# Where the steps of the mixers' generators are cut: behind each product's operands instead of behind its result

## The chip, the cores and the metric

The kernel runs on one core of a Trainium2 chip. The metric is the device time of one execution in microseconds; the median of three runs of the kernel before is 2840.65 us (2838.29 to 2842.82).

## What is computed

Two transformer-like blocks, one behind the other, on 1024 tokens of width 1024, in float32. The first block has three mixers beside each other, the second has two; each block ends with a feed-forward part. Cut to what matters here:

```python
def first_block(x, meta_tokens, w_in, ..., w_mlp_in, w_mlp_out, ln2_g, ln2_b):
    h = jnp.concatenate([meta, x], axis=1)                  # 16 + 1024 tokens
    proj = h @ w_in[l]
    q_a, f_a, i_a, g_a, z_b, xbc_b, dt_b, u_c = jnp.split(proj, split_idx, axis=-1)
    y_a = hgrn2_mixer(q_a, f_a, i_a, g_a, ...)              # 6 heads, a scan over chunks
    y_b = mamba2_mixer(z_b, xbc_b, dt_b, ...)               # 6 heads, a scan over chunks
    y_c = s5_mixer(u_c, ...)                                # complex diagonal scan, then a gate
    mixed = jnp.concatenate([y_a, y_b, y_c], axis=-1) @ w_out[l]
    h = layer_norm(ALPHA * h + mixed, ln1_g[l], ln1_b[l])
    ff = jnp.square(jax.nn.relu(h @ w_mlp_in[l])) @ w_mlp_out[l]
    h = layer_norm(ALPHA * h + ff, ln2_g[l], ln2_b[l])
    return h[:, N_META:]

def second_block(x, w_in, ...):
    qkv, z, beta_logit, a, sg_uv, gates = jnp.split(x @ w_in[l], pts, axis=-1)
    o_a = deltanet_branch(qkv, z, beta_logit, a, ...)       # gated delta rule, 4 heads
    o_b = spatial_gating_branch(sg_uv, ...)                 # 128-token blocks, 4 groups
    h = gate_a * (o_a @ w_branch_a[l]) + gate_b * (o_b @ w_branch_b[l])
    x = layer_norm_2(DEEPNORM_ALPHA * x + h @ w_out[l], ln1_g[l], ln1_b[l])
    up = causal_depthwise_conv_2(x @ w_up[l], conv_ffn[l])
    a_ff, b_ff = jnp.split(up, 2, axis=-1)
    return layer_norm_2(DEEPNORM_ALPHA * x + (jax.nn.silu(a_ff) * b_ff) @ w_down[l], ln2_g[l], ln2_b[l])
```

## The kernel before, in words

**Tiling.** Tokens are handled in two halves of 512 (the first with the 16 meta tokens in front). A dense product is made of 128 x 128 blocks of the stationary operand and 512 columns of the moving one, and each float32 product is three matmuls of high and low parts (`mm3`, line 233). A block of weights of 128 x 1024 comes in on SyncE's queue (`weights`, line 223): two buffers for the raw block, three each for the high part `wh` (made on ScalarE) and the low part `wl` (made on VectorE). The sums are in four PSUM banks called `ps`. The mixers have four PSUM banks of their own, `px` (`bank`, line 177), and 24 working tiles `f` (`t`, line 165).

**Generators.** Everything is written as Python generators: a dense part yields after each unit (24 matmuls of 512 columns where a tile is made, 12 where a down projection adds up), a mixer yields after each of its steps. `steps` (line 1553) runs a dense generator and puts steps of a mixer's generator among its own: after each dense step the pace `r` is added to a debt, and for each whole unit of debt one mixer step is issued. So with a pace below one some dense steps have no mixer step behind them, and with a pace above one several mixer steps come one right behind the other. `both` (line 1454) makes one step out of one step of each of several generators.

**The mixers' steps.** `hgrn` (line 354) goes over seven block sizes; for each one VectorE and ScalarE make an operand `M`, TensorE multiplies it, and the result is copied under a mask into the scores; then it yields. It yields nine times per pair of heads. `mamba` (line 564) yields after each of seven convolutions, twice for each chunk, and three times in its norm. `delta` (line 983) yields 18 times per head: among these, six times for the doubling of a triangular inverse (product, copy by ScalarE, product, masked copies by VectorE), twice for its refinement (product, VectorE, product, VectorE), and four times for the chain over the chunks (product, VectorE, product, ScalarE, product). `spatial` (line 1154) yields four times. Two heads of `delta` run in turns.

**Where they run.** HGRN2 and Mamba2 of the first half run beside S5 and beside the first projection `p1` (lines 1488 to 1490), and of the second half beside the first output projection and the first feed-forward part (lines 1497 and 1504). The delta rule and the spatial gate run beside the second block's projection `p2` and then beside a feed-forward part (lines 1517 and 1519 for the first half, 1534 and 1536 for the second).

**The order on an engine.** The calls give the program's order. When the tile context closes, a planner turns it into one list for each engine: it goes by program order but may take a later instruction first while an earlier one waits for its operands. [...]

The functions that the diff touches follow; `square` and `sums` (lines 537 and 546) make the two parts of a square and add them up over partitions by a product with ones.

Of the kernel before, what the change touches and what calls it, by code (L numbers as in the profile page):

```python
# [17 lines left out]
DRAM = bass.MemoryType.DRAM  # L18
# [11 lines left out]
# columns of the constant array  # L30
C_ID = 0
C_I10 = 128                   # 1024 times the identity
C_SGN = C_I10 + 128
C_TRI = C_SGN + 1
C_BLK = C_TRI + 128           # ones in the two diagonal 64-blocks
C_BAND = C_BLK + 128          # 64 zeros, 128 ones, 64 zeros
C_N = C_BAND + 256

# columns of the array of byte masks: the levels (only the columns in the second halves of their blocks),
# the same transposed (only the first halves), the diagonal, what is below it  # L40
# [6 lines left out]
# columns of the per-feature parameter array  # L47
P_HNW = 0
P_LB = 1
P_CW1 = P_LB + 3              # 7 x 4  # L50
# [4 lines left out]
P_CWQ = P_GB + 2              # 12 x 4  # L55
P_DNW = P_CWQ + 48
P_CWF = P_DNW + 1             # 44 x 3
# [4 lines left out]
# columns of the row array (the same on all partitions)  # L62
# [7 lines left out]
# order of the feature-major tiles of the first projection  # L70
U1 = dict(u=0, f=2, q=5, g=8, xbc=11, z=18)
NU1 = 21
# ... and of the second
# [4 lines left out]
class Op:  # L78
    """The hi and lo parts of an operand."""
# [8 lines left out]
class Kb:  # L88
# [54 lines left out]
    def mask(self, o, b=None):  # L143
        """A byte mask for four blocks of 128 columns, or for the halves of a level's blocks in them."""
        n = 128
        if b is not None:
            o += 64 * LEVELS.index(b)
            n = 64
        m = self.bm[:, o:o + n].rearrange("p (o t) -> p o t", o=1).to_broadcast([128, 4, n])
        return m if b is None else m.rearrange("p c (n b) -> p c n b", b=b)  # L150

    def halves(self, x, i, b):
        """The first or second halves of the blocks of 2 b columns."""
# [11 lines left out]
    def t(self, w, dt=F32):  # L165
        """A working tile of the mixers."""
        return self.mx.tile([128, 528], dt, tag="f", bufs=self.NF, name=self.nm("f"))[:, :w]

    def ta(self):
        """Two working tiles of 528 columns, out of the accumulators' tiles."""  # L170
# [16 lines left out]
    # ---------------------------------------------------------------- operands  # L187
# [18 lines left out]
    def xt(self, f=False):  # L206
        """A tile for the hi and lo parts of an operand; f: out of the mixers' tiles."""
# [8 lines left out]
    def split(self, src, w, f=False):  # L216
        """hi and lo parts of src [128, w]."""
# [5 lines left out]
    def weights(self, src, w):  # L223
        """hi and lo parts of a block of weights [128, w] in DRAM."""
# [8 lines left out]
    def mm3(self, out, a, b, start, stop):  # L233
        """out += a^T b with hi and lo parts."""
# [4 lines left out]
    def fm(self, out, w, xs, o, n, k0=0):  # L239
        """out [128 features, n tokens] from a unit of weights and the tiles xs."""  # L240
# [5 lines left out]
    # ---------------------------------------------------------------- first projection  # L246
# [91 lines left out]
    # ---------------------------------------------------------------- HGRN2  # L338
    def hgrn_pre(self):
        """ln(1 - lb) and lb, a column for each pair of heads."""  # L340
# [13 lines left out]
    def hgrn(self, p, h):  # L354
# [13 lines left out]
        # log f and k  # L368
# [19 lines left out]
        # scores  # L388
# [17 lines left out]
        # the queries of a level for both heads at once, each among zeros for the other's features  # L406
# [3 lines left out]
        for i, b in enumerate((16, 8, 4, 2, 1, 64, 32)):  # L410
# [11 lines left out]
            if b <= 16:  # L422
# [3 lines left out]
                for hd, o in ((0, 0), (1, 64)):  # L426
                    self.tt(y4[o:o + 64, :, hd, :].rearrange("p c (n b) -> p c n b", b=b), c5(M, o), c5(q, o), ALU.mult)
                ps = self.bank()
# [6 lines left out]
            else:  # L435
                self.tt(M4[:, :, 1, :], M4[:, :, 1, :], q4[:, :, 1, :], ALU.mult)

                def put(S, ps):
                    for j in range(0, 128, 2 * b):
                        self.act(S[j:j + b, :, j + b:j + 2 * b], ps[j:j + b, :, j + b:j + 2 * b])  # L440
                scores(M, M, b, put)
            yield
            if b == 1:
                di = self.mask(M_ID)
                scores(q, kr, 0, lambda S, ps: nc.vector.copy_predicated(out=S, mask=di, data=ps))
        yield
        # decays
# [12 lines left out]
        # kd with tokens on the partitions, and what each chunk adds to the state  # L460
# [5 lines left out]
        dS = self.bank().rearrange("p (c d) -> p c d", d=64)  # L466
        if h == 0:
# [3 lines left out]
            self.act(kTm[:16], b[:16, :128])  # L471
            for o in (0, 64):
# [4 lines left out]
        # the states before the chunks, both heads' on the diagonal  # L477
# [12 lines left out]
        self.hs[p] = last  # L490
        o_ = self.bank()
# [5 lines left out]
        yield  # L497
        # norm and gate
        g = self.t(512)
        nc.sync.dma_start(g, self.S1["g", p, h][:, 3 + R0:3 + NT])  # L500
        self.act(g, g, AF.Silu)
        ms = self.bank()
        self.sums(ms, [(self.blk, self.square(o_), slice(0, 128))])
# [7 lines left out]
    # ---------------------------------------------------------------- Mamba2  # L511
    def softplus(self, x, tag, w):
        """max(x, 0) + ln(1 + exp(-|x|)) in place; x is narrow."""
# [6 lines left out]
    def rows(self, x, n):  # L520
        """The sums over tokens up to each, a row in DRAM for each of the n columns of x."""
# [15 lines left out]
    def square(self, x):  # L537
        """The hi and lo parts of the square of x [128, 512]."""
# [7 lines left out]
    def sums(self, out, parts):  # L546
        """The sum of the products of ones (lhsT) and operands (p: their partitions)."""
# [4 lines left out]
    def conv4(self, src, NT, cw, cb, out):  # L552
        """Causal convolution of four taps, then silu."""
# [10 lines left out]
    def mamba(self, h):  # L564
# [8 lines left out]
        # dt and dA, with tokens on the partitions; the first six columns are the short chunk  # L573
        dt = self.s("m2dt", 30)
        d3 = dt.rearrange("p (c h) -> p c h", h=6)
        if h == 0:
# [9 lines left out]
                self.m2a.rearrange("p (o h) -> p o h", o=1).to_broadcast([128, 5 - c0, 6]), ALU.mult)  # L586
        b = self.bank()
# [5 lines left out]
        for c in range(c0, 5):  # L593
            L = 16 if c == 0 else 128
            t0 = 0 if c == 0 else R0 + 128 * (c - 1)
            # acum_t and exp(acum_t) on all partitions
# [24 lines left out]
            # x dt and B with tokens on the partitions  # L621
# [39 lines left out]
        # gate, norm  # L661
        sq = []
        for j in range(3):
# [4 lines left out]
            sq.append(self.square(Y[j]))  # L668
# [1045 lines left out]
```

## Time and profile before

| | us |
|---|---|
| median of three runs | 2840.65 |
| span of the profiled execution, first to last instruction | 2831.3 |
| TensorE matmul busy | 2768.6 (98%) |
| TensorE weight loads busy | 2262.4 (80%) |
| VectorE busy | 1793.7 (63%) |
| ScalarE busy | 1163.4 (41%) |
| GpSimd busy | 220.4 (8%) |

The profile gives no time for its own execution other than the span; the median of the runs is 9.4 us longer than this span. Names in its rows are the program's: `ps` and `px` are the two sets of PSUM banks, `f` a mixer's working tile, `xt` an activation in its two parts, `wh` and `wl` the parts of a block of weights, `ta` a tile of S5. Line 204 is the helper that issues every matmul, line 189 every activation, line 192 every two-operand VectorE instruction, so these are told apart by their tiles.

### The profile page before, as it was taken

To read this page: it belongs to the slowest core of one execution; us is meant where nothing else is said; L and a number is where in the kernel's file an instruction comes from. 1 tells how busy PE (TensorE), PEld (TensorE's weight loads), DVE (VectorE), ACT (ScalarE), POOL (GpSimd) and SP (SyncE) were. 2 spreads that over 40 slices of the span, in tenths; PEclk is the share of its full clock that TensorE was granted. 3 is DMA by queue.
4 is the path that set the end of the run, shared out by engine and by line. 5 is a ranking of instruction groups with operands and counts; after the bars stand their busy time and mean duration, and the time that the engine had idled before them with its cause. 6 is when DMAs were issued, how large, how long until landed. Compare 5 with 4: busy or idle time off the path is not lost.

```text
span 2831.3 us, 37337 instructions
## 1 busy us (share of the span) xinstructions
PE 2768.6 (98%) x14176; PEld 2262.4 (80%) x14176; DVE 1793.7 (63%) x3321; ACT 1163.4 (41%) x1810; POOL 220.4 (8%) x365
## 2 busy tenths in 40 slices
PE   8999999999999999999999999999999999999997
PEld 7788777777878878877788888888788888888886
DVE  7678768777756554386545675535867557675556
ACT  4334344444442353364323334435545334344432
POOL 3121000000001121010000001110100000000000
PEclk9999999999999999999999999999999999999999
DMA  7333462323344444333333455433244433342232
GB/s 220 122 94 93 139 202 81 113 89 113 106 147 149 157 144 133 123 101 123 105 104 119 142 184 166 126 126 130 79 136 140 149 104 101 107 139 92 97 96 75
DMA packets 138036, 351.55 MB, mean 124 GB/s; under 512 B 26779, under 2 KB 40641, under 8 KB 137857
## 3 DMA queue, kind: packets, MB, share of 16 engines
q1 hardware_dynamic: 113712, 295.34, 32.9%
q0 software_dynamic: 16672, 48.50, 5.0%
q10 hardware_dynamic: 7473, 5.34, 0.7%
q8 instruction: 111, 1.82, 0.3%
q14 instruction: 68, 0.56, 0.1%
HBM read 296.84 MB, written 51.69 MB: 123 GB/s over the span
## 4 chain that ended last, share of the span: by engine, by line
PE 81%; issue 7%; DVE 6%; DMA 2%; ACT 2%; POOL 1%; SPq 0%; DVEq 0%; POOLq 0%; ACTq 0%
PE ps L204 73%; PE px L204 7%; DVE f L192 2%; ACT f L189 1%; DVE wl L192 1%; PE px L1265 1%; DVE f L195 1%; DMA hx<-ev 1%; DMA wr<-in_w 0%; DVE acc L195 0%; DMA f<-rows 0%; DVE f L433 0%; ACT wh L189 0%; DVE ta L192 0%; ACT ev L189 0%
## 5 line engine op out<-in xcount | busy, mean ns | idle before, releaser
L204 PE MATMUL ps<-xt,wh 128*128 128x512 f32 (+1 forms) x3616 | 1117.0, 388 | 8.7 <-ACT wh L189 8.5
L192 DVE TENSOR_TENSOR wl<-wr,wh 128x1024 fp32r<-128x1024 f32 (+3 forms) x431 | 521.5, 1210 | 606.7 <-ACT wh L189 590.2
L189 ACT ACTIVATE wh<-wr 128x1024 fp32r<-128x1024 f32 (+3 forms) x431 | 452.3, 1050 | 898.4 <-PE ps L204 826.1
L204 PE MATMUL ps<-wh,xt 128*128 128x512 f32 (+3 forms) x2624 | 813.1, 384 | 4.7 <-ACT xt L189 4.4
L204 PEld LDWEIGHTS ps<-xt,wh 128*128 128x128 f32 x3616 | 665.9, 189 | 141.7 <-ACT wh L189 8.5
L204 PE MATMUL ps<-xt,wl 128*128 128x512 f32 (+1 forms) x1808 | 698.6, 387 | 3.9 <-DVE wl L192 3.9
L204 PEld LDWEIGHTS ps<-wh,xt 128*128 128x128 f32 (+1 forms) x2624 | 485.8, 188 | 99.9 <-ACT xt L189 6.9
L204 PE MATMUL ps<-wl,xt 128*128 128x512 f32 (+3 forms) x1312 | 502.2, 383 | 0.8 <-DVE wl L192 0.7
L204 PEld LDWEIGHTS ps<-xt,wl 128*128 128x128 f32 x1808 | 341.5, 189 | 72.8 <-DVE wl L192 5.5
L204 PE MATMUL ps<-f,wh 128*128 128x512 f32 x960 | 300.5, 394 | 0.0
L204 PEld LDWEIGHTS ps<-wl,xt 128*128 128x128 f32 (+1 forms) x1312 | 246.7, 188 | 46.5 <-DVE wl L192 2.0
L189 ACT ACTIVATE f<-f 128x512 f32<-128x512 f32 (+6 forms) x300 | 178.5, 613 | 200.6 <-DVE f L192 62.3
L204 PE MATMUL px<-f,f 128*128 128x128 f32 (+8 forms) x1832 | 201.4, 258 | 16.8 <-DVE f L192 10.2
L204 PEld LDWEIGHTS ps<-f,wh 128*128 128x128 f32 x960 | 180.3, 188 | 42.3
L189 ACT ACTIVATE ev<-ps 128x512 f32<-128x512 f32 (+4 forms) x303 | 169.6, 561 | 72.9 <-PE ps L204 67.1
L192 DVE TENSOR_TENSOR acc<-acc,ps 128x512 f32<-128x512 f32 x192 | 130.8, 683 | 95.8 <-PE ps L204 93.9
L204 PE MATMUL ps<-f,wl 128*128 128x512 f32 x480 | 189.4, 394 | 0.0
L204 PEld LDWEIGHTS px<-f,f 128*128 128x128 f32 (+2 forms) x1192 | 133.3, 180 | 52.9 <-issue 22.8
L192 DVE TENSOR_TENSOR f<-f,f 128x256 f32<-128x256 f32 (+5 forms) x244 | 128.6, 547 | 39.0 <-ACT f L189 37.0
L189 ACT ACTIVATE xt<-ev 128x512 fp32r<-128x512 f32 x131 | 82.3, 629 | 149.2 <-DVE ev L192 145.9
L195 DVE SCALAR_TENSOR_TENSOR ev<-ev,p,ev 128x512 f32<-128x512 f32 x176 | 132.2, 751 | 2.7 <-ACT ev L189 0.6
L192 DVE TENSOR_TENSOR xt<-ev,xt 128x512 fp32r<-128x512 f32 x124 | 85.9, 696 | 49.6 <-ACT xt L189 49.1
(223 smaller groups left out, 2046.9 us busy)
## 6 DMA issues: line engine op xcount, KB each, us to landing
wr<-in_w SPq DMA_DIRECT2D x93, 512.0 KB, 3.8
wr<-in_wup SPq DMA_DIRECT2D x88, 512.0 KB, 3.5
wr<-in_wmi SPq DMA_DIRECT2D x64, 512.0 KB, 3.6
wr<-in_wmo SPq DMA_DIRECT2D x64, 512.0 KB, 3.6
wr<-in_wdn SPq DMA_DIRECT2D x44, 512.0 KB, 3.5
wr<-in_wo SPq DMA_DIRECT2D x32, 512.0 KB, 3.7
Y<-f POOLq DMA_DIRECT2D x32, 256.0 KB, 2.6
ev<-Y SPq DMA_DIRECT2D x32, 256.0 KB, 3.6
```

The costliest lines, as they stand in the source:

```text
L189: self.nc.scalar.activation(out=out, in_=in_, func=func, **kw)
L192: self.nc.vector.tensor_tensor(out=out, in0=a, in1=b, op=op)
L195: self.nc.vector.scalar_tensor_tensor(out=out, in0=a, scalar=s, in1=b, op0=op0, op1=op1)
L204: self.nc.tensor.matmul(out, lhsT, rhs, start=start, stop=stop)
L1265: nc.tensor.transpose(b[:, 128 * t:128 * t + 128], acc[t][:, 128 * k:128 * k + 128], self.ident)
```

## The change

The yields are moved so that a mixer step begins with matmuls whose operands an earlier step made and ends with the VectorE and ScalarE work that makes the operands of the next one. Steps that held two or three dependent products are cut between them. The paces are raised in proportion to the new number of steps. No instruction is added or removed; some are issued earlier in program order (the squares of a norm, the row load and exponentials of `delta`, one product of the diagonal in `hgrn`). The diff also takes out comments and doc strings, which shifts line numbers and is left out here.

```diff
 def hgrn(self, p, h):
     for i, b in enumerate((16, 8, 4, 2, 1, 64, 32)):
         ...                                   # makes M (and y)
             if b <= 16:
+                yield
                 ps = self.bank()
                 ...                           # 4 products, masked copies
             else:
                 ...
+                yield
                 scores(M, M, b, put)
-            yield
-            if b == 1:
+            if i == 0:
                 di = self.mask(M_ID)
                 scores(q, kr, 0, ...)
-        yield
         ...                                   # decays, kd, qe
         self.tt(qe, q, eG[:, R0:NT], ALU.mult)
+        yield
         ...                                   # kd transposed into kT
-        dS = self.bank().rearrange("p (c d) -> p c d", d=64)
         if h == 0:
             ...
             self.act(kTm[:16], b[:16, :128])
+        yield
+        dS = self.bank().rearrange("p (c d) -> p c d", d=64)
+        if h == 0:
             for o in (0, 64):
                 self.mm(dS[o:o + 64, 0, :], kTm[:16, o:o + 64], vm[:16, o:o + 64])
         ...                                   # dS, the states S
         self.hs[p] = last
+        yield
         o_ = self.bank()
         ...                                   # products into o_
-        yield
         g = self.t(512)
         nc.sync.dma_start(g, ...)
         self.act(g, g, AF.Silu)
+        sq = self.square(o_)
+        yield
         ms = self.bank()
-        self.sums(ms, [(self.blk, self.square(o_), slice(0, 128))])
+        self.sums(ms, [(self.blk, sq, slice(0, 128))])
 def mamba(self, h):
     ...                                       # dt, dA
+        yield
         b = self.bank()
         self.mm(b[:, 0:30 - 6 * c0], self.tri, dA[:, wd])
     ...                                       # all chunks; gate and squares of the norm
+        yield
         for j in range(3):
             ...
 def glu(self, h):
     ...                                       # loads, gelu
+        yield
         for m in range(2):
 def delta(self, hd, h, cols):
     ...                                       # three convolutions
+        sq = [self.square(x) for x in (q, k)]
         yield
         ...                                   # norms of q and k, from sq
-        yield
         ...                                   # rows loaded, E, eR
         self.act(E, E, AF.Exp)
+        yield
         ...                                   # k and v transposed
-        yield
         ...                                   # k k^T, k q^T with decay
         yield
         ...
         for lb in (2, 4, 8, 16, 32, 64):
             ...
             self.act(self.halves(Z, 0, lb), nb(b))
+            yield
             ...                               # two products, masked copies
             yield
         for _ in range(2):
             ...
             self.stt(c3(R16), c3(b), 1024.0, k1024, mult, add)
+            yield
             ...
             yield
         for c in range(4):
             if S is not None:
                 self.mm(b[:, 0:128], k[:, s], S)
                 self.tt(R, vt[:, s], b[:, 0:128], sub)
+                yield
             b = self.bank()
             self.mm(b[:, 0:128], XT[:, s], R)
             self.act(u, b[:, 0:128], AF.Copy, scale=col(be, c))
+            yield
             ...
             yield
         self.act(z, z, AF.Silu)
+        sq = self.square(o)
+        yield
         ...                                   # sums from sq, norm, gate
 def spatial(self, h):
     for t in range(4):
         ...                                   # gelu, norm of v
+            yield
         ...                                   # 4 products, bias and gate into u
+            yield
         ...                                   # 4 transposes, copy, store
-            yield
 def run(self):
-        st(p1, 3, m, 2.7)
-        st(p1, 10, m, 3)
-        st(p1, 99, m, 3, False)
+        st(p1, 3, m, 3.1)
+        st(p1, 10, m, 3.5)
+        st(p1, 99, m, 3.5, False)
-        st(self.out_proj(ys, ap["wo1"], a0), 99, m, 0.75, False)
+        st(self.out_proj(ys, ap["wo1"], a0), 99, m, 0.9, False)
-        st(q, 76, m, 0.6, False)
+        st(q, 76, m, 0.72, False)
-        st(p, 99, m, 0.6, False)               # beside p2, both halves
+        st(p, 99, m, 1.15, False)
-        st(q, 80, m, 0.8, False)
+        st(q, 80, m, 1.5, False)
-        st(q, 36, m, 1, False)
+        st(q, 36, m, 1.9, False)
```

## Rows read from the trace of the kernel before

**Rows 1.** The page: span, then busy time, share and instructions of each engine.
```profile
span 2831.3 us, 37337 instructions
PE 2768.6 (98%) x14176; PEld 2262.4 (80%) x14176; DVE 1793.7 (63%) x3321; ACT 1163.4 (41%) x1810; POOL 220.4 (8%) x365
```
**Rows 2.** TensorE groups by shape, 2200 to 2800 us: count | busy us, mean ns | idle before.
```profile
L204 PE MATMUL ps<-xt,wh 128*128 128x512 f32 x288 | 90.1, 394 | 0.0
...
L1265 PE MATMUL px<-c,acc 128*128 128x128 f32 x32 | 4.6, 272 | 0.0
```
**Rows 3.** Window 2200 to 2800: us, busy (count) of PE, PEld, DVE, ACT, POOL; PEclk, DMA.
```profile
2200.00:2800.00 600.00, 599.96 (x2604) 485.50 (x2603) 370.35 (x551) 244.00 (x322) 9.12 (x16) 1.00 0.33 108
```
**Rows 4.** TensorE's waits, 105 to 400 us: waited for: us in total, times, longest.
```profile
PE px L204 <- DVE f L192: 9.3, 7, 2.8
PE px L204 <- POOL f L479: 1.9, 1, 1.9
```
**Rows 5.** TensorE's waits, 1040 to 1365 us.
```profile
PE px L204 <- ACT f L189: 1.9, 2, 1.1
PE px L1044 <- DVE f L195: 1.2, 1, 1.2
```
**Rows 6.** TensorE's waits, 1785 to 2145 us.
```profile
PE px L204 <- ACT f L189: 3.2, 5, 1.2
PE px L1044 <- DVE f L195: 1.1, 1, 1.1
```
**Rows 7.** TensorE groups by shape, 105 to 400 us.
```profile
L204 PE MATMUL ps<-xt,wh 128*128 128x512 f32 x382 | 125.0, 403 | 0.0
...
L204 PE MATMUL px<-f,f 128*128 128x128 f32 x160 | 26.1, 298 | 7.0 <-DVE f L192 3.7 <-POOL f L479 1.9 <-ACT ev L189 1.4
```
**Rows 8.** TensorE groups by shape, 480 to 830 us.
```profile
L204 PE MATMUL ps<-xt,wh 128*128 128x512 f32 x453 | 143.9, 397 | 0.0
L204 PE MATMUL ps<-wh,xt 128*128 128x512 f32 x384 | 124.6, 398 | 0.0
...
L204 PE MATMUL px<-f,f 128*128 128x128 f32 x120 | 19.0, 286 | 1.2 <-DVE f L192 1.2
```
**Rows 9.** TensorE groups by shape, 1040 to 1365 us.
```profile
L204 PE MATMUL ps<-xt,wh 128*128 128x512 f32 x501 | 167.9, 403 | 0.0
...
L204 PE MATMUL ps<-wh,xt 128*128 128x512 f32 x149 | 51.4, 409 | 0.0
L204 PE MATMUL px<-f,f 128*128 128x128 f32 x224 | 34.0, 282 | 0.2 <-DVE f L195 0.2
```
**Rows 10.** TensorE groups by shape, 1785 to 2145 us.
```profile
L204 PE MATMUL ps<-xt,wh 128*128 128x512 f32 x618 | 203.9, 402 | 0.0
...
L204 PE MATMUL ps<-wh,xt 128*128 128x512 f32 x128 | 44.1, 411 | 0.3 <-DVE acc L195 0.3
...
L204 PE MATMUL px<-f,f 128*128 128x128 f32 x216 | 33.3, 281 | 0.0
```
**Rows 11.** Windows, columns as in rows 3, PEclk the third from the right.
```profile
100.00:125.00 25.00, 22.48 (x98) 18.26 (x98) 17.89 (x48) 12.12 (x22) 4.16 (x8) 0.93 0.44 135
250.00:275.00 25.00, 24.45 (x220) 21.08 (x218) 24.07 (x80) 10.57 (x23) 2.16 (x4) 1.00 0.21 62
275.00:300.00 25.00, 23.14 (x106) 17.98 (x106) 17.14 (x42) 9.66 (x16) 3.16 (x6) 0.86 0.32 107
```
**Rows 12.** Timeline of TensorE, first scores of HGRN2: start, us, what, [idle before].
```profile
117.50 0.68 PE L204 MATMUL px<-f,f 128*128 128x128 f32 x4 [2.49 <-DVE f L192]
```
**Rows 13.** Timeline of TensorE around a norm's sums in HGRN2.
```profile
602.51 0.39 PE L204 MATMUL px<-f,o 128*128 128x512 f32 x1
602.74 0.39 PE L204 MATMUL ps<-xt,wh 128*128 128x512 f32 x1
602.97 0.40 PE L204 MATMUL px<-f,o 128*128 128x512 f32 x1
```
**Rows 14.** All engines' waits, whole span: ScalarE's on the mixers' products.
```profile
ACT f L189 <- PE px L204: 110.6, 77, 5.0
```

More of the change, by code (lines that the diff above doesn't have):

```diff
@@ L992, in delta @@
             self.conv4(self.S2["qkv", j, h][:, 0:515], 512, P_CWQ + 4 * j, None, x)
+        sq = [self.square(x) for x in (q, k)]
         yield
-        for x, bias in ((q, self.lnq), (k, 0.0)):
+        for x, y, bias in ((q, sq[0], self.lnq), (k, sq[1], 0.0)):
             b = self.bank()
-            self.sums(b, [(self.ones, self.square(x), slice(0, 128))])
+            self.sums(b, [(self.ones, y, slice(0, 128))])
             r = self.t(512)
@@ L1118, in delta @@
         self.act(z, z, AF.Silu)
+        sq = self.square(o)
+        yield
         b = self.bank()
-        self.sums(b, [(self.ones, self.square(o), slice(0, 128))])
+        self.sums(b, [(self.ones, sq, slice(0, 128))])
         r = self.t(512)
@@ L1533, in run @@
         st(n)
-        st(p, 99, m, 0.6, False)
+        st(p, 99, m, 1.15, False)
         q = self.ffn(0, x0, a0, ((0, 4), (4, 4), (8, 4), (12, 4), (16, 4), (20, 2)))
-        st(q, 36, m, 1, False)
+        st(q, 36, m, 1.9, False)
         st(m)
```

## The prediction

> **What bounds the kernel now.** I read the engine table first: TensorE is busy for 2768.6 of 2831.3 us, every other engine far less [rows 1]. So only time in which TensorE waits can be won; the change takes no matmul away. The span is 9.4 us under the median of the runs, 2840.65; I work in differences and put them on the median.
>
> Next, a stretch without mixers, as the measure of an undisturbed TensorE: from 2200 to 2800 us a 512-column matmul has a mean of 394 ns, a 128-column one in a mixer's bank 272, and no idle time [rows 2]; 2604 of them in 600 us is one in 0.23 us [rows 3]. (Matmuls overlap, so these durations are compared with each other and not added up.) Then the four stretches in which mixers run beside dense work, by the view of TensorE's waits and by the groups of matmuls: A, 105 to 400 us (HGRN2, Mamba2, S5 beside the first projection); B, 480 to 830 (HGRN2 and Mamba2 of the second half); C, 1040 to 1365, and D, 1785 to 2145 (delta rule and spatial gate, for each half).
>
> The waits that the profile names before a mixer's matmul (`px`), for an operand that VectorE, ScalarE or GpSimd was still making, are 9.3 + 1.9 = 11.2 us in A [rows 4], 1.2 in B [rows 8], 3.1 in C [rows 5] and 4.3 in D [rows 6]: 19.8 us.
>
> [...]
>
> [...] Against 394 ns, in A the group of 382 has 403; each pair of matmuls with a high part has one with the low part, so I take one and a half times: 9 ns x 382 x 1.5 = 5.2 us [rows 7]. B: (3 x 453 + 4 x 384) x 1.5 = 4.3 us [rows 8]. C: (9 x 501 + 15 x 149) x 1.5 = 10.1 us [rows 9]. D: (8 x 618 + 17 x 128) x 1.5 = 10.7 us [rows 10]. In the mixers' own 128-column products, against 272: A 26 x 160 = 4.2, B 14 x 120 = 1.7, C 10 x 224 = 2.2, D 9 x 216 = 1.9 us [rows 7 to 10].
>
> On the mixers' side (waits, clock, long products) the ceiling is therefore A 11.2 + 5.2 + 4.2 = 20.6, B 2.9, C 5.3, D 6.2: 35 us. On the dense side it is 5.2 + 4.3 + 10.1 + 10.7 = 30 us.
>
> [...]
>
> **The change, part by part.** No instruction is added, and the order of dependent instructions stays. What moves is how much dense work stands between a mixer's operand and its product.
>
> Steps counted by the yields: `hgrn` 9 to 11, `mamba` 20 to 22 (second half 17 to 19), `glu` 2 to 3, `delta` 18 to 33 (34 in the second half), `spatial` 4 to 8. So HGRN2 with Mamba2 has 47 to 55 steps, the second half with its gate 46 to 55, the delta rule's two pairs with the spatial gate 40 to 74 and 76. The paces go up by 1.15 to 1.17, 1.2, and 1.88 to 1.92. The mixers end where they ended: in A after 13 dense steps 38 of 47 steps are out, now 44 of 55, and both need some three dense steps more; in B after about 66 dense steps of the feed-forward part, as now. So no tail is made and none goes, and that part costs nothing.
>
> The gain depends on the pace. With a pace below one each mixer step stands alone between dense steps, and an operand made at the end of one step has at least one dense step (12 or 24 matmuls of 0.23 us, 2.8 to 5.5 us [rows 3]) before its product. With a pace of 3.5 three or four steps follow each other and only the first has dense work in front.
>
> B (0.9 and 0.72): all steps alone. All of the 2.9 us go, and of the dense side's 4.3 I take half, because some dense waits are ScalarE and VectorE being late by the same bursts: 5 us.
>
> C: beside `p2` the pace is 1.15, six of seven steps alone; beside the feed-forward part 1.5, half alone. I take 0.7 of 5.3, and 0.2 of 10.1 on the dense side, whose weights are made by the same two engines as before: 3.7 + 2.0 = 5.7 us.
>
> D: 1.15 and then 1.9, where nine in ten steps come in pairs, and a pair of half steps is an old step. Half of 6.2, and 0.1 of 10.7: 3.1 + 1.1 = 4 us.
>
> A: 3.1 to 3.5, one step in 3.5 has dense work in front: 20.6 x 0.29 = 6 us.
>
> Against this in A: S5 has as many steps as before but is drawn along faster, 3.5 for 3 a dense step. VectorE is busy for 24.07 of 25 us at 250 to 275 us [rows 11] and has no room for a sixth more of S5 there; some of it runs over. Bounds: nothing if it slides into the next window, at 17.14 of 25 us with 7.9 free [rows 11]; at worst the sixth of 24.07, 4 us, at one place, and S5 has four such passes, 16 us. I take 2, near the lower end, because the room is in the very next row.
>
> Moved instructions: squares, the row load of `delta` on ScalarE's queue and its exponentials, the diagonal product of `hgrn` are issued one step earlier. Behind each stands the making of the next weights, covered by the three `wh` and `wl` buffers; if that cover is gone a late block costs its ScalarE and VectorE time. Tiles are held one step longer, two parts for each of q and k in two heads: 8 of the 24 `f`, at a point where six others are held. Bounds: 0 to one wait as long as the 1.9 us for a tile of GpSimd [rows 4]. I take 0.
>
> Sum: -(5 + 5.7 + 4 + 6) + 2 = -18.7 us, so 2840.65 - 18.7 = 2822 us. The bounds of these choices are 2836 (only B gains) and 2791 (all of the mixers' side, 35, and half of the dense side, 15); the forecast's own range is 2803 to 2834, twice the gain to a third of it.
>
> **Rivals.**
> First, the planner already does this (no change). It takes dense matmuls between two dependent products: a product of the norm at 602.51 us, a dense matmul at 602.74, the next product at 602.97 [rows 13]. Then moving the yields only changes which of equal choices is taken, and only B, whose paces are below one, gains its 5 us: 2836. Against it: the planner let a wait of 2.49 us stand [rows 12], so its idea of when an operand is ready is short, and dense work between gives room for that.
>
> Second, slower: the extra step ends hold up the weights. Each product's result is taken out by ScalarE or VectorE, and ScalarE waited 77 times for such a product, 110.6 us in all, 1.44 us each [rows 14]. Such a wait is harmless while the three weight buffers are ahead. The change has 8 + 9 + 34 + 36 = 87 more rounds of mixer steps, at each of which a weight block may stand behind the wait. If a round costs a quarter of that wait, 0.36 us, that is 31 us against a gain of 19: 2853. It decides from 0.22 us a round. For it: dense matmuls are the slower ones in C and D already. Against it: in pairs the new ends stand where the old insides stood.
>
> [...]
>
> Third, more: waits go almost wholly, because most of the gain is in the planner being given any dense work at all: 2840.65 - 35 - 15 = 2791.
>
> **Chances.** Forecast 0.60, no change 0.16, slower 0.14, more 0.10. 0.2%, 5.7 us, is about what a measurement of this kernel can tell from no change: faster means under 2835, slower over 2846. The forecast and the third rival are faster, 0.70; the first rival lies at the edge and is counted as the same, with a little more from the second, 0.15; the rest, 0.15, slower. The range leaves out the far ends of the second and third rival, some 0.07 and 0.05: 2795 to 2848.
>
> **What would show it.** Right: in the waits view the sums before `px` in A to D fall from 19.8 us to under 10; the granted clock has no dip near 117 us; the mean of the 512-column groups in B falls towards 394; C falls more than D. The 1.9 pace shows by D's products with 64 columns still in pairs. Wrong: if waits of dense matmuls for `wh` or `wl` grow, the second rival; if VectorE is over 24 us in several windows of 25 between 150 and 300 us, S5's bunching; if the means of C and D stay within 2 ns, the planner did it already. The time at which the out projection starts should move by no more than A gains.

## The result, and the profile after

The changed kernel is slower: 2854.86 us (median, 2849.02 to 2855.16) against 2840.22 beside it, 1.0051 of before with an interval of 1.0034 to 1.0068, or +14.6 us. I had forecast 2822. The second rival's 2853 is near in size, but its mechanism isn't what happened, as the runs below show.

The page of after, span and busy times, columns as in [rows 1]:
```profile
span 2853.4 us, 37338 instructions
PE 2777.1 (97%) x14176; PEld 2277.1 (80%) x14176; DVE 1790.9 (63%) x3321; ACT 1161.4 (41%) x1810; POOL 220.2 (8%) x365
```
The work is the same, and the span is 22.1 us longer, more than the 14.6 us of the medians: executions of one kernel lie several us apart (the four of after by 6.1), and the profiled one of before is a short one. So the traces tell where, and the ratios how much.

TensorE's waits in after, at 105 to 400 us, at 400 to 440, at 480 to 830 and at 1040 to 1365 (columns as in [rows 4]):
```profile
PE px L204 <- DVE f L192: 9.5, 6, 3.4
PE px L204 <- ACT f L189: 5.6, 2, 5.1
...
PE px L204 <- ACT f L189: 8.4, 2, 5.3
...
PE px L204 <- DVE f L192: 2.9, 3, 1.8
...
PE px L204 <- ACT f L189: 3.1, 4, 1.7
PE ps L204 <- DVE wl L192: 1.1, 2, 0.6
```
In A the two largest kinds of wait before `px` sum to 15.1 us, for 11.2 [rows 4], instead of falling. Behind A, at 400 to 440, 8.4 us stand before `px`, where before had 0.9, and 4.4 before dense matmuls:
```profile
PE ps L204 <- ACT xt L189: 4.4, 3, 3.1
PE px L204 <- ACT f L189: 0.9, 1, 0.9
```
B has 2.9 for 1.2 [rows 8], C 3.1 behind ScalarE for 1.9 [rows 5].

The groups of 512 columns in A and C of after (as in [rows 7, 9]):
```profile
L204 PE MATMUL ps<-xt,wh 128*128 128x512 f32 x387 | 124.6, 400 | 0.0
...
L204 PE MATMUL ps<-xt,wh 128*128 128x512 f32 x518 | 167.6, 399 | 0.0
```
In A, C and D 403, 403 and 402 ns became 400, 399 and 398; in B 397 and 398 became 399 and 401. These longer means are not the short waits that I had taken them for. TensorE's timeline of before, in C:
```profile
1117.57 0.52 PE L204 MATMUL px<-f,f 128*128 128x64 f16 x12
1117.93 0.47 PE L204 MATMUL ps<-xt,wh 128*128 128x512 f32 x1
1118.24 0.39 PE L204 MATMUL ps<-xt,wl 128*128 128x512 f32 x1
```
The dense matmul directly behind a mixer's product lasts 0.47 us, though nothing is waited for, and the next starts 0.31 us behind it; the one behind a dense matmul lasts 0.39. Counted over C of before, the 851 dense matmuls of 512 columns behind a dense one have a mean of 394 ns, as in the stretch without mixers [rows 2], and the 124 behind a mixer's product 469. In after these are 884 at 395 and 84 at 481. So what fell is how often TensorE changes from a mixer's products to dense work.

In these two traces most of the time is lost by the end of the first half. Dense matmuls done in the first 500 us, before and after (window, PE busy, count of `ps` matmuls, clock):
```profile
0.00:500.00 500.00, 365.17 (x1777) 0.97 0.45 137
```
```profile
0.00:500.00 500.00, 349.79 (x1715) 0.95 0.45 134
```
After is 62 behind, 14 us at one in 0.23 us [rows 3]; 38 of them are lost between 400 and 500 us. At 830 us it is 78 behind, at 2300, 95.

What happens there is the end of the first projection. Its 1512 dense matmuls are followed by 36 of the output projection that need only HGRN2's output; the next needs Mamba2's, and later ones the output of S5's gate. (My expectations call all 1548 the first projection's.) TensorE's timeline there (start, us, what), first before, then after:
```profile
418.69 0.40 PE L204 MATMUL ps<-wh,xt 128*128 128x512 f32 x1
420.01 3.70 PE L204 MATMUL px<-f,f 128*128 128x512 f32 x8 [0.92 <-ACT f L189]
423.15 0.79 PE L204 MATMUL ps<-wh,xt 128*128 128x512 f32 x1
```
```profile
425.28 0.40 PE L204 MATMUL ps<-wh,xt 128*128 128x512 f32 x1
425.51 1.11 PE L204 MATMUL px<-f,o 128*128 128x512 f32 x4
431.88 6.35 PE L204 MATMUL px<-f,f 128*128 128x512 f32 x8 [5.25 <-ACT f L189]
437.66 0.80 PE L204 MATMUL ps<-wh,xt 128*128 128x512 f32 x1
```
Between the last of the 1548 and the next dense matmul before has 4.5 us (418.69 to 423.15), after 12.4 (425.28 to 437.66). The last four of the sums of Mamba2's norm, which before lie between dense matmuls of the 36 (at 409.65 and 410.94), now come behind them all, and the gate's eight matmuls, alone in both, wait 5.25 us for 0.92. They take 6.35 us for 3.70, and the granted clock is 0.57 over 430 to 438 us, as the window of after shows (columns as in [rows 3]); at 418.7 to 423.2 of before it is 1.00:
```profile
430.00:438.00 8.00, 6.12 (x9) 2.62 (x9) 2.05 (x3) 2.77 (x5) 0.95 (x2) 0.57 0.94 285
```

GpSimd's timeline has Mamba2's last write and the gate's last write, first before, then after:
```profile
416.14 0.54 POOL L683 DMA_DIRECT2D Y<-f  x1 [1.02 <-DVE f L195]
...
427.00 0.54 POOL L947 DMA_DIRECT2D Y<-f  x1 [1.14 <-DVE f L199]
```
```profile
430.96 0.54 POOL L690 DMA_DIRECT2D Y<-f  x1 [0.55 <-DVE f L195]
...
442.33 0.54 POOL L955 DMA_DIRECT2D Y<-f  x1 [0.92 <-DVE f L199]
```
Both are some 15 us later. HGRN2 was late already. The dense matmuls done when its second and third pair are written (window, PE busy, count of `ps` matmuls, clock), before and after:
```profile
0.00:229.60 229.60, 176.95 (x969) 0.99 0.49 145
0.00:290.90 290.90, 217.41 (x1168) 0.98 0.43 129
```
```profile
0.00:251.60 251.60, 191.13 (x1049) 0.98 0.49 139
0.00:324.20 324.20, 239.57 (x1262) 0.97 0.44 127
```
Pair two is 80 dense matmuls later, pair three 94. The question for the runs was why, and what the rest of the change does.

### The profile page after: what moved, and what is told of

The parts are those of the page before. It is cut to its first block, busy times and chain, and to the rows that moved or that the text cites. A ratio compares the mean times of both kernels' runs of the same rounds, so it can differ in the third digit from the quotient of the medians.

```text
span 2853.4 us, 37338 instructions
## 1 busy us (share of the span) xinstructions
PE 2777.1 (97%) x14176; PEld 2277.1 (80%) x14176; DVE 1790.9 (63%) x3321; ACT 1161.4 (41%) x1810; POOL 220.2 (8%) x365
## 4 chain that ended last, share of the span: by engine, by line
PE 78%; issue 9%; DVE 6%; DMA 4%; ACT 2%; POOL 1%; SPq 0%; DVEq 0%; POOLq 0%; ACTq 0%
PE ps L204 71%; PE px L204 6%; DVE f L192 1%; ACT f L189 1%; DVE wl L192 1%; PE px L1280 1%; DVE f L195 1%; DMA ev<-gt 1%; DMA f<-rows 1%; DVE acc L195 1%; DMA wr<-in_w 1%; DMA cx<-qkv 1%; ACT ev L189 0%; DVE ta L192 0%; DVE f L434 0%
## 5 line engine op out<-in xcount | busy, mean ns | idle before, releaser
L204 PE MATMUL ps<-xt,wh 128*128 128x512 f32 (+1 forms) x3616 | 1105.1, 387 | 8.8 <-ACT wh L189 8.6
L192 DVE TENSOR_TENSOR f<-f,f 64x256 f32<-64x256 f32 (+5 forms) x244 | 128.5, 546 | 31.5 <-ACT f L189 30.6
```

Source lines behind the costliest of these rows:

```text
L192: self.nc.vector.tensor_tensor(out=out, in0=a, in1=b, op=op)
L204: self.nc.tensor.matmul(out, lhsT, rhs, start=start, stop=stop)
```

## Experiments

All ratios are against runs of the kernel before on the same chip, with five rounds; 0.1% is 2.8 us.

### Which block

Run e1 has the second block's hunks of the diff alone, e2 the first block's.

> Only the second block's part of the change: delta and spatial with the new step ends and their paces of 1.15, 1.5, 1.15 and 1.9; the first block as before. Theory (the loss is made at the first projection, with HGRN2 and Mamba2): at most +4 us on the kernel before, 2841 to 2845, with C and D together between -2 and +5 at the end of the span and nothing before 1040 us. Rival (the step ends hold up the weights wherever they stand, so the loss goes with their number, 70 of 87 rounds being here): +12 us, 2852.

Measured: 1.0002 (0.9993 to 1.001).

> Only the first block's part: hgrn, mamba and glu with the new step ends, paces 3.1 and 3.5 beside the first projection and 0.9 and 0.72 in the second half; the second block as before. Theory: nearly the whole loss, +12 to +18 us, 2853 to 2858, and there by 440 us. Rival (loss with the number of rounds, 17 of 87): +3 us, 2843.

Measured: 1.0046 (1.0034 to 1.0058). The loss is the first block's. My second rival's cost of 0.36 us for each round would be 25 us for the 70 of 87 rounds that are in the second block, far more than the 9.7 us of gain that I had forecast there could hide; e1 excludes it.

### Which half, and is it the pace

```diff
 # e4: as e2, old paces           # e5: no step end moved, new paces
-st(p1, 10, m, 3.5)               -st(p1, 10, m, 3)
+st(p1, 10, m, 3)                 +st(p1, 10, m, 3.5)
 # e6: as e2, 3.4 and 3.9         # e7: new hgrn, mamba, glu if h == 1; e8: if h == 0
```


> As the run of the first block's part, but with the old paces 2.7 and 3 beside the first projection: the finer steps are drawn more slowly and S5 as before. If the faster drawing of S5 and of Mamba2, whose chunks were not cut, makes the loss: within 4 us of the kernel before at 440 us, 2838 to 2845. If the finer step ends themselves make it (another order of the same work): +10 or more, 2851 and over.

> The kernel before with only the paces 3.1 and 3.5 beside the first projection; no step end is moved. If the faster drawing makes the loss: +8 to +16 us, 2849 to 2857, with most of it at 350 to 440 us. If the finer step ends make it: within 4 us of before, 2837 to 2845, since the mixers then only end earlier.

> The first block's part (its step ends, 0.9 and 0.72 in the second half), but 3.4 and 3.9 beside the first projection in place of 3.1 and 3.5, so that HGRN2's second and third pair leave at about the dense matmul where they left before (969 and 1168, against 1049 and 1262). Theory (the paces leave the mixers late: the first projection's matmuls, 1548, are used up before Mamba2's norm and S5's gate): the tail goes, and with it 7 of the 13 us; 0.999 to 1.003 of the kernel before, with the last write of the gate at dense matmul 1563 or before. Rival (the step ends themselves cost, wherever the mixers end): 1.004 to 1.007, as before this change of paces.

> The new step ends of hgrn, mamba and glu in the second half alone, beside the out projection and the feed-forward part, with 0.9 and 0.72; the first half has the old steps and paces. Theory (the loss is in the first half, at the end of the first projection): 0.999 to 1.0015 of before. My prediction had -5 us here, 0.998. Rival (the step ends cost wherever they stand): +3 to +6 us, 1.001 to 1.002, all of it between 505 and 840 us.

> The other part: the new step ends in the first half alone with 3.1 and 3.5, the second half as before. Theory: +8 to +13 us, 1.003 to 1.0046 of before, with the mixers' last write at or after dense matmul 1563 and waits of over 8 us in all before px between 367 and 424 us. Rival (the loss lies in the second half): 1.001 or less.

Measured: e4 1.0057 (1.0046 to 1.0068), e5 1.0008 (0.9999 to 1.0017), e6 1.0059 (1.0047 to 1.0072), e7 1.0026 (1.0017 to 1.0035), e8 1.004 (1.0028 to 1.0052).

My first theory, faster drawing of S5 and Mamba2, fell with e4 and e5: the new paces alone do almost nothing, the new step ends at the old paces lose as much. The second, mixers that only leave late because the pace is short, fell with e6: at 3.9 the pairs still leave at 1049 and 1243. In after, e2, e4, e6 and e8 67 to 71 us pass between the writes of pair one and pair two (50 before), at whatever pace. So the first half is most of the loss, the second half has a smaller one of its own (the two sum to 0.66%, more than e2's 0.46), and something other than the pace makes HGRN2 slow.

### S5 in turns

`both` draws one step of S5 for each step of HGRN2 or Mamba2. HGRN2 has 11 steps for 9 now, S5 as many as before: between two writes of HGRN2 stand two more S5 steps. Runs e10 to e12 change that ratio alone:

```diff
-    def both(self, *gs):
+    def both(self, *gs, r=None):     # gs[0] is drawn r times in a round
-        m = self.both(m, self.seq(0))
+        m = self.both(m, self.seq(0), r=...)   # e10: as e8, 9/11; e11: old steps, 11/9; e12: old steps, 0.9
```


> The mirror: the kernel before, no step end moved, but S5 drawn 11 times in 9 rounds. Theory: HGRN2's second and third pair leave later (over 1000 and 1200), Mamba2's last write at dense matmul 1545 or later, 1.002 to 1.005 of before. Rival: 1.000 within 0.001.

Measured: 1.0026 (1.0016 to 1.0037), with no step end moved. The pairs leave at 1053 and 1251, as in after, and Mamba2's last write is at 1548. VectorE's work on S5's tiles (`ta`) between the writes of pair one and pair two (window, busy, count; the rest is clock and DMA), for before, after, e11 and e10:
```profile
180.00:229.60 49.60, 14.74 (x60) 1.00 0.34 107
```
```profile
180.20:251.60 71.40, 27.98 (x110) 1.00 0.33 94
```
```profile
181.30:247.70 66.40, 22.39 (x78) 1.00 0.31 93
```
```profile
179.90:226.90 47.00, 9.45 (x49) 1.00 0.32 104
```
In after VectorE does 28 us of S5 in that interval for 14.7, 13 more, and the interval is 71.4 us for 49.6, 22 more. S5 itself is done early for it; its last writes to `yT` begin at 346.98 for 373.60.

> The new step ends in the first half alone with 3.1 and 3.5 (1.0040 of before in the run of the first half), but S5, which takes turns with HGRN2 and Mamba2, is drawn 9 times in 11 rounds in place of 11, since HGRN2 has 11 steps for 9. Theory (the turns, one for one, put S5's long VectorE work ahead of HGRN2 and Mamba2, which then end late): HGRN2's pairs leave at dense matmuls near 969 and 1168 again, no wait over 3 us before px between 367 and 432 us, 0.999 to 1.0015. Rival (the step ends in HGRN2 and Mamba2 lengthen their own chain, S5 or not): pairs still at 1049 and 1262, 1.003 to 1.005.

Measured: 1.0032 (1.0019 to 1.0045). The pairs are back at 980 and 1198 and the interval at 47 us, so the turns are what made HGRN2 late. The time is back by little: S5's last writes are now at 390.95, and Mamba2 and the gate end at 419 and 430 us, still 3 us later than in before. (The profiled execution is the fastest of the five, 2.8 us under their median, so its trace shows less than the ratio.) Half of this expectation is wrong: with S5's old place HGRN2 is in time again, and the time is not.

> The kernel before with S5 drawn 9 times in 10 rounds. Theory: HGRN2 and Mamba2 end earlier in dense matmuls and their tail shrinks, 0.997 to 1.000, unless S5, now last, holds the gate: then 1.001 to 1.003 with the gate's loads late. Rival (the turns do not matter): 1.000 within 0.001.

Measured: 0.9951 (0.9936 to 0.9965), 14 us faster than before with one ratio changed. Mamba2's last write and the gate's in e12:
```profile
387.88 0.54 POOL L683 DMA_DIRECT2D Y<-f  x1 [1.52 <-DVE f L195]
...
404.52 0.54 POOL L947 DMA_DIRECT2D Y<-f  x1 [2.00 <-DVE f L199]
```
Windows 100 to 440 us (PE, PEld, DVE, ACT, POOL; then the granted clock), before, after and e12:
```profile
100.00:440.00 340.00, 320.45 (x2005) 267.58 (x2005) 245.49 (x634) 142.54 (x269) 46.59 (x88) 0.97 0.42 129
```
```profile
100.00:440.00 340.00, 314.58 (x1956) 262.83 (x1956) 241.51 (x623) 136.42 (x257) 43.25 (x82) 0.95 0.42 125
```
```profile
100.00:440.00 340.00, 328.46 (x2074) 274.69 (x2073) 259.37 (x672) 148.72 (x276) 46.68 (x88) 0.99 0.44 132
```
In the same 340 us e12 gets 69 matmuls more done than before, after 49 fewer. The granted clock differs as well, a mean of 0.97, 0.95 and 0.99 in before, after and e12; as an estimate, 0.02 of 340 us is 7 us, or 30 matmuls at one in 0.23 us [rows 3], on either side.

### The tail itself

Run e9 moves the gate of the first half forward, into S5's generator.

```diff
         for q in range(4):
             yield from self.s5(q)
+        yield from self.glu(0)
...
-        st(self.glu(0))
```


> The kernel before with S5's gate (glu of the first half) behind S5 in the same generator, so that it runs beside the first projection and not behind Mamba2; nothing else. Theory (what follows the last dense matmul of the first projection is an uncovered chain, Mamba2's norm and then the gate): -3 to -8 us, 0.997 to 0.999 of before, with the gate's two writes before dense matmul 1500 and the out projection starting right after Mamba2's writes. Rival (the tail is covered by the out projection's own matmuls and the weights ahead of it): 1.000 within 0.001.

Measured: 1.0048 (1.0036 to 1.006); I had the sign wrong. The gate is written before 397 us, but Mamba2's last write is at 432.33 for 416.14. ScalarE's timeline (its DMA queue as ACTq) in e9, lines of the gate and of Mamba2:
```profile
382.45 0.63 ACT L189 ACTIVATE f<-f 128x512 f32<-128x512 f32 x1 [3.33 <-DMA f<-yT]
...
389.29 0.69 ACT L189 ACTIVATE f<-px,s5gb 128x512 f32<-128x512 f32 x1 [2.87 <-PE px L204]
...
393.36 0.69 ACT L189 ACTIVATE f<-px,s5gb 128x512 f32<-128x512 f32 x1 [2.44 <-PE px L204]
...
394.94 0.33 ACTq L602 DMA_DIRECT2D f<-rows  x1
```
The first row load of Mamba2's last chunk, issued from ScalarE's queue, is at 394.94; before has it at 373.89. In front of it ScalarE waited 3.33, 2.87 and 2.44 us for the gate's loads and products, 8.6 of the 21 us; the rest went to the gate's own work, to weights and results, and to waits for those. In the trace the load stands behind these three waits, which it doesn't need. It is the same fault as S5's turns: work that nobody waits for yet, put ahead of the chain that ends last.

### Do the first half's step ends cost or pay by themselves

Runs e15 and e17 are e8 with S5 drawn at 0.74 and 0.78; e18 has the new `mamba` and `glu` alone in the first half, old paces, S5 at 0.9.

> The new step ends in the first half with 3.1 and 3.5, S5 drawn 74 times in 100 rounds: 0.9 of the 9/11 that keep its place beside HGRN2. If the step ends themselves pay once S5 is out of the way, as I predicted (6 us): 0.993 to 0.9945 of before, under the 0.9951 of S5 at 0.9 with the old steps. If they neither pay nor cost: 0.995 to 0.9965. If they cost by themselves: 0.998 or more.

> The new step ends in the first half with 3.1 and 3.5, S5 drawn 78 times in 100 rounds, between the runs at 9/11 (1.0032, Mamba2 last) and at 0.74 (0.9999, S5 last). If only the balance counts: 0.995 to 0.997, as S5 at 0.9 with the old steps, with both chains ended before dense matmul 1500. If the step ends lengthen the mixers' own chain, HGRN2 and Mamba2 can't end early and S5 too: 0.9985 to 1.002, with Mamba2's or the gate's last write after 1540.

> S5 drawn 9 times in 10 rounds and the old paces, with the new step ends of mamba and glu in the first half, hgrn as before. If HGRN2's step ends are what makes the mixers late: 0.995 to 0.997 of the kernel before, as without any. If those of Mamba2 and the gate do it as well, being nearest to the end: 0.998 to 1.001.

Measured: e15 0.9999 (0.999 to 1.0008), e17 0.9983 (0.9974 to 0.9991), e18 1.0007 (0.9998 to 1.0016). S5's last writes and the gate's last write in e15 and e17, and the gate's in e18:
```profile
407.61 3.68 SPq L926 DMA_DIRECT2D yT<-ta  x8
...
423.43 1.07 POOL L1741 DMA_DIRECT2D Y<-f  x2 [17.66 <-DVE f L199]
```
```profile
386.67 3.66 SPq L926 DMA_DIRECT2D yT<-ta  x8
...
411.61 0.54 POOL L1741 DMA_DIRECT2D Y<-f  x1 [1.11 <-DVE f L199]
```
```profile
420.29 0.54 POOL L1741 DMA_DIRECT2D Y<-f  x1 [1.33 <-DVE f L199]
```
At 0.74 S5 is last, at 9/11 Mamba2; at 0.78, the best of the three, the gate still ends 7 us after that of e12. So the step ends don't pay here at any of the three ratios: e12, with the old ones, is 0.3% faster than e17. e18 shows that those of Mamba2 and the gate, nearest to the end, are enough to lose 0.56% on e12; at the old paces their three extra steps also come one dense step later, so it doesn't tell a longer chain from a later one. That a chain cut into more steps takes longer, because each cut puts dense matmuls between a product and what uses it, fits both runs, but was not shown by itself.

### The second half

e14 is e7 with 0.8 and 0.66.

> The new step ends in the second half alone, with 0.8 and 0.66 in place of 0.9 and 0.72. If the 0.26% lost there come from one place where steps happen to meet (waits of 1.83 and 0.63 us before px at 639 to 643 us and a granted clock of 0.83 over the ten us behind): another pace moves the meeting, and the time is 0.999 to 1.001 of before. If every step end costs: 1.0015 to 1.0035 again.

Measured: 1.0006 (0.9996 to 1.0016). Windows 635 to 655 us of before, e7 and e14 (columns as in [rows 3], granted clock third from the right):
```profile
635.00:655.00 20.00, 19.58 (x140) 15.66 (x139) 16.83 (x29) 7.43 (x13) 0.00 (x0) 1.00 0.25 77
```
```profile
635.00:655.00 20.00, 17.37 (x119) 13.76 (x118) 18.45 (x37) 6.98 (x12) 0.00 (x0) 0.91 0.26 79
```
```profile
635.00:655.00 20.00, 20.00 (x115) 16.58 (x115) 19.78 (x47) 7.11 (x11) 0.00 (x0) 1.00 0.12 36
```
In e7 TensorE is idle for 2.6 us there, for 0.4 in before, and the granted clock is 0.91 for 1.00, as an estimate 20 x 0.09 = 1.8 us more: some 4 of the 7 us by which e7 is slower. The rest isn't located. With other paces the place is gone, and the time is that of before within 0.16%; that this one place was the whole cause isn't shown. The gain of 5 us that I had for this part isn't there either, although the waits before `px` in B do fall in e14, to 0.3 us for 1.2 [rows 8].

### The second block at lower paces

```diff
-        st(q, 80, m, 1.5, False)
+        st(q, 80, m, 0.72, False)     # e3; e1 has 1.5
-        st(q, 36, m, 1.9, False)
+        st(q, 36, m, 1.25, False)     # e3; e1 has 1.9
```


> The second block's part with lower paces where the changed kernel has 1.5 and 1.9: 0.72 beside the feed-forward part of 80 steps and 1.25 beside the one of 36, 1.15 beside the projections as before. Theory (steps that come in pairs give back what single steps gain: about 5 + 3 us gained beside the projections, 7 lost behind them): -4 to -8 us, 0.997 to 0.9985 of the kernel before. Rival (the step ends cost nothing and gain nothing whatever the pace): 1.000 within 0.001, as with 1.5 and 1.9.

Measured: 0.9973 (0.9961 to 0.9985), 7.6 us faster than before. C in two windows, beside `p2` and beside the feed-forward part, of before, e1 and e3:
```profile
1040.00:1200.00 160.00, 157.73 (x947) 132.21 (x947) 63.58 (x105) 57.90 (x101) 21.36 (x34) 1.00 0.38 125
1200.00:1365.00 165.00, 163.14 (x930) 129.41 (x929) 120.95 (x214) 84.98 (x146) 16.84 (x20) 1.00 0.36 117
```
```profile
1040.00:1200.00 160.00, 160.00 (x939) 135.95 (x939) 64.95 (x100) 61.10 (x102) 16.35 (x30) 1.00 0.41 133
1200.00:1365.00 165.00, 159.70 (x896) 128.77 (x895) 106.99 (x195) 72.11 (x125) 15.55 (x18) 0.97 0.33 107
```
```profile
1040.00:1200.00 160.00, 160.00 (x945) 135.99 (x944) 64.88 (x103) 62.14 (x107) 18.79 (x34) 1.00 0.41 130
1200.00:1365.00 165.00, 163.35 (x902) 133.18 (x901) 97.35 (x159) 63.87 (x106) 6.66 (x8) 0.99 0.27 85
```
Beside `p2`, at 1.15, TensorE's idle time of 2.3 us goes to nothing. Behind it, at 1.5, it is 5.3 us for 1.9 and the clock 0.97; at 0.72, with the mixers drawn out beyond this window, it is 1.7. In C pairs of new half steps are worse than the old steps, single ones aren't. In D, behind `p2`, both are worse: 3.6 us idle at 1.9 and 4.0 at 1.25, for 2.3.

In all, idle time in C and D falls by 3.0 us in e3 (8.7 to 5.7), less than half of the 7.6. Another difference is the number of changes from mixers to dense work. Dense matmuls directly behind a product into `px`, counted from 830 to 2400 us, are 292 in before, 227 in e1 and 205 in e3; the next one starts 0.315 us behind such a matmul (median) and 0.23 behind others. As an estimate, 87 fewer times 0.08 us are 7 us, which with the idle time is 10 and enough for the 7.6. In e1, 65 fewer are 5 us, and the clock of 0.97, by the same kind of estimate 165 x 0.03 = 5 us, would take them back. No run changes this number alone, so it isn't shown as the cause.

### Together

Run e13 is e12 and e3 together, e16 the same with S5 at 0.85.

> The two parts that gained, together: S5 drawn 9 times in 10 rounds in the first half (old steps of hgrn, mamba and glu), and the second block's new step ends with 1.15, 0.72, 1.15 and 1.25. If they lie in different stretches and add up: 0.9951 and 0.9973 give 0.9924, 0.991 to 0.994 of the kernel before.

> As the two parts together, with S5 at 0.85 in place of 0.9, so that it ends some two rounds behind Mamba2. If Mamba2 still sets when the out projection can start: 0.002 to 0.004 under the run with 0.9. If S5's gate does now: the same or up to 0.003 over it.

Measured: e13 0.9933 (0.9919 to 0.9947), 2809.7 us against 2828.9, faster than both kernels; e16 0.9987 (0.9977 to 0.9997). They add up nearly. In e16 S5's last writes begin at 398.46 for 381.00 in e12 and the gate's at 419.39 for 404.52: 0.85 is already too slow, and on that side S5 is the chain that ends last.

## Why the prediction was wrong, point by point

**The step that failed:** "The mixers end where they ended ... So no tail is made and none goes, and that part costs nothing." I counted steps up to the end of the list and got the same place. But the place in the list is not when the chain ends. S5's turns put 13 us more of its VectorE work into one interval of HGRN2, HGRN2's third pair left 94 dense matmuls later, and the end of Mamba2's norm and the gate came after the dense work was used up. With A and S5's term I had -4 us for the first half; it measured 1.0040 (e8), some +11 us. The turns alone cost 0.26% with the old step ends (e11). With the new ones, S5's old place beside HGRN2 gives back only 0.08% (e10), and the best ratio tried stays 0.3% behind the old step ends (e17 and e12). So the new step ends cost something of their own in the first half; through what, stays open.

**S5.** I saw that it is drawn along faster and looked for room on VectorE, +2 us. Room was the wrong question: the pace alone costs at most 0.17% (e5, 1.0008), the ratio of S5's steps to HGRN2's moves the time both ways (e11, 1.0026, and e12, 0.9951).

**A, -6 us.** The waits did not fall. My 11.2 us left out 2.9 that the view also names before `px` (1.4 for ScalarE's `ev`, 0.6 for its `f`, 0.9 for VectorE's `ta`), and in C I left out 0.9. In full they are 14.1, 1.2, 4.0 and 4.3 us in A to D of before and 16.2, 2.9, 4.7 and 5.4 in after. (B is without 5.5 us at line 1295, which in before, as line 1280, fall in front of 480 us.) The long one before HGRN2's first scores is still there (2.61 us, for 2.49 in [rows 12]), and e15 and e17 show no pay from these step ends even with S5 moved. The 5.2 us for the clock in A's 20.6 are 25 x 0.07 and 25 x 0.14, from the 0.93 and 0.86 of [rows 11]; that earlier operands win them back no run shows: in after the granted clock is 0.90 at 100 to 125 us, and over 105 to 400 us it is 0.96 for 0.98.

**The dense side.** I took means above 394 ns, and above 272 in the mixers' own products, for short waits. In the traces the longer dense matmuls stand directly behind the mixers' products (469 ns for 394 in C of before; single ones 0.79 us at 423.15 and 0.47 at 1117.93), with nothing waited for, and in A some ran at a lower granted clock (0.63 us at 282.13, at 0.50 over 282.1 to 282.8). That this is waiting time which an earlier operand would win back, no run shows: the means of the mixers' 128-column products, 298, 286, 282 and 281 ns in A to D [rows 7 to 10], are 308, 295, 276 and 276 in after.

**B, -5 us.** Measured +0.26% in e7, of which one place with its clock dip is more than half, and 1.0006 at other paces. In e14 the named waits went as forecast, and it was worth nothing that can be measured: 1.2 us are too few. The dense half of the term had nothing to give: TensorE changes from mixers to dense work 47 times in B, and 45 and 47 times in e7 and e14.

**C and D, -5.7 and -4.** e1 has 1.0002 in all. The idle time goes beside `p2`, but pairs at 1.5, to which I gave a smaller gain, lose in C. The 7.6 us of e3 are near my 9.7 by luck: those terms were for 1.5 and 1.9, and what fits e3 as well is fewer changes between mixers and dense work, which I didn't have.

Against the forecast the first half is off by some 15 us, the second half by 12 (e7) and the second block by 10 (e1); these sum to 37, where the whole change is off by 33 (+14.6 for -18.7).

**Rivals.** The second, weights held up, came near the time by accident: e1, with most of the rounds, loses nothing. TensorE's waits for `wl` did grow in C, from none to 1.1 us, which is small. The first, that the planner does it already, had B alone gain 5 us, and B gains nothing. None of the rivals had the chain that ends at a point where dense work runs out; "the time at which the out projection starts" stood only as a sign to look at.

## What to carry to other kernels

Where generators take turns, cutting one of them into more steps changes every ratio between them: count, for each chain, what the engines do ahead of it, and find the point where the dense work that covers it runs out. Here it paid to draw the chain that ends last faster than the others, a little (e12), until another one ended last (e16). New step ends paid in the second block at low paces (e3), paid nothing there in pairs (e1), and paid nowhere in the first block: not singly (e7, e14), and with several behind each other not either, once S5's turns are set for both (e17 against e12). Before you take a longer mean for waiting, look at what stands in front of the longer ones.

## What the runs showed that I had not expected

In e7, 2.6 us idle at 635 to 655 us went with a granted clock of 0.91 over the 20 us, for 0.4 and 1.00 in before: as an estimate another 1.8 us (20 x 0.09). And the order is fragile: three edits that each seemed harmless (e9 and e11 against before, e18 against e12) moved the time by 0.3 to 0.6%, and in each Mamba2 or the gate ended at another time. At a change from mixers to dense work the next dense matmul started some 0.08 us later than elsewhere (0.315 us behind the first one for 0.23, medians over 830 to 2400 us), at nearly all of them with nothing waited for.
